# An encoder trunk on one core: the S5 scan in chunks of 16 tokens instead of 8, with values, gates and queries placed anew

## The chip, the cores and the metric

The kernel runs on one core of a Trainium2 chip. The metric is the device time of one execution in microseconds, the median of several runs. A core has a matrix engine (TensorE, PE in the profile, with PEld for its weight loads), three engines for elementwise work (VectorE, DVE; ScalarE, ACT; GpSimd, POOL) and SyncE (SP), which here only issues transfers. Transfers are issued from the queues of SP and POOL.

## The reference

One layer of a hybrid encoder runs over 2304 tokens: two sequences of 256 and 2048 tokens, each scanned on its own. All data is float32.

```
h = rmsnorm(x, norm1_g);  q, zf_f, zf_b, vi, g, u = split(h @ w_in)      # 1024 -> 3072
ya = hgrn2(q, zf_f, zf_b, vi, g)          # 4 heads of 128, gated linear recurrence, both directions
# S5: u in 32 groups of 16 channels, 64 complex states per group, both directions
bu = u @ Bbar;  x_t = Abar * x_{t-1} + bu_t;  y = Re(C x_fwd) + Re(C x_bwd) + d*u
z = gelu(y);  yb = norm(z * sigmoid(z @ glu_w + glu_b)) * merge_g
x = x + concat(ya, yb) @ w_out
x = rmsnorm(x + relu(rmsnorm(x) @ w_ff1)**2 @ w_ff2)
```

## The kernel before

Tokens go in six blocks of 384. A float32 product is made of three products of split operands (hi x hi, hi x lo, lo x hi; `mm3`, lines 174 to 179); the S5 and table products are plain float32 matmuls, which show as two passes each. The order of the instructions on each engine is set when the kernel is built: a planner simulates the engines and always takes the ready instruction that comes first in the program, so that later work can fill a hole of earlier work. `order` adds an edge that holds one instruction behind another; `hold[0]` does so for every `tt` on VectorE that is traced while it is set.

Stage 1 (lines 499 to 537) loads x, norms and transposes a block (`stage1_norm`), stores h split in two halves to DRAM, and projects u (`stage1_proj`, four output tiles of 128 channels per block, each 24 matmuls of 384 columns). `s5_tables` (277 to 497) works out on VectorE the powers of Abar and, in eight calls of `quad` for four groups each, three tables that go through DRAM: `win_d` (u to chunk-end state; transposed on TensorE), `wc_d` (state to output) and `k_d` (u to output inside a chunk, 15 lags; products of `bb` and `wc` on TensorE, line 486). A chunk is LC = 8 tokens, so that a matmul contracts 8 x 16 channels = 128 rows and its columns are the 288 chunks. `QD` says behind which block's norm which calls of `quad` stand. Of the values only block 5 is projected here (V1 = 5).

The entry of the scan (583, `s5_in`): for each of 32 groups two matmuls (real and imaginary), 128 rows, 288 columns, forward and backward states in two halves of the output partitions, copied by ACT (forward) and DVE (backward) into the state tiles `stt_`. The scan (589 to 595): in each round `s5_step` runs once for each direction, three VectorE operations a step: a product with `adec`, and two sums. For the first 30 rounds a step handles both sequences at once. Beside the scan run the values of blocks 0 to 4 (`stage2_v`, h loaded again by `load_h`), then gates and queries of blocks 0 to 3 (`stage2_gq`, eight units of 24 matmuls per block). The exit (638 to 658) makes, for each group, three matmuls of 288 columns into one bank: the table `tm` from `k_d` on u, and two of `wc` on the copied states `xg`; ACT evacuates, POOL stores.

Then the gate stage (716 to 763): gelu on ACT and DVE, a GLU product per block, with gates and queries of blocks 4 and 5 (`late`) placed between by `LN`. The gated recurrence, the output projection and the MLP follow and are the same in both kernels.

Of the kernel before, what the change touches and what calls it, by code (L numbers as in the profile page):

```python
# [9 lines left out]
F32 = mybir.dt.float32  # L10
# [24 lines left out]
JP = NPROMPT // LC  # L35
# [9 lines left out]
def hybrid_trunk_kernel(  # L45
# [80 lines left out]
    win_d = [dram.tile([P, 4, P], F32, name=f"win_d{i}") for i in range(G // 2)]  # L126
    wc_d = [dram.tile([P, 2, 4, LC * C16], F32, name=f"wc_d{o}") for o in range(8)]
    k_d = [dram.tile([4, C16, 15 * C16], F32, name=f"k_d{o}") for o in range(8)]
# [52 lines left out]
    def proj_fm(o, wu, hh, hl):  # L181
        for k in range(KD):
            mm3(o, wu[0][:, k], wu[1][:, k], hh[k // 4][:, k % 4], hl[k // 4][:, k % 4], k == 0, k == KD - 1)
# [74 lines left out]
    def stage1_proj(b):  # L258
        hh, hl = hx[b]
        for f in range(4):  # L260
            pu = ptile("mm", TB)
            proj_fm(pu, uw[f], hh, hl)
            ut = tmp.tile([P, LC, JB], F32, name="ut", tag="ut")
            act(ut, pu.rearrange("p (j i) -> p i j", i=LC), AF.Copy)
            GP.dma_start(out=u_d[f].rearrange("i f j -> f i j")[:, :, b * JB:(b + 1) * JB], in_=ut)

# [10 lines left out]
    def s5_tables():  # L277
        GQ = 4
# [78 lines left out]
        ap = par.tile([P, 2, 10, G], F32, name="apow")  # L357
# [21 lines left out]
        pw1 = par.tile([P, 4, G], F32, name="pw1")  # L379
        pw2 = par.tile([P, 4, G], F32, name="pw2")  # L380
# [7 lines left out]
        adec = []  # L388
        for d in range(2):
            ad = const.tile([P, 2, 2, G // 2], F32, name=f"adec{d}")  # L390
            for q in range(2):
                o, i = ad[q * 64:(q + 1) * 64], ap[d * 64:(d + 1) * 64, :, LC, q::2]
# [4 lines left out]
            adec.append(ad)  # L397
# [19 lines left out]
        pin = par.tile([P, 2, G, LC], F32, name="pin")  # L417
        for i in range(LC):
            V.tensor_copy(out=pin[:64, :, :, i], in_=ap[:64, :, LC - 1 - i, :])
            V.tensor_copy(out=pin[64:, :, :, i], in_=ap[64:, :, i, :])  # L420
        pout = par.tile([P, 2, G, 10], F32, name="pout")
        for e in range(10):
            V.tensor_copy(out=pout[:64, :, :, e], in_=ap[:64, :, 9 - e, :])
            V.tensor_copy(out=pout[64:, :, :, e], in_=ap[64:, :, e, :])

        dcol = par.tile([32, G // 2], F32, name="dcol")
        nc.sync.dma_start(out=dcol, in_=s5_d[0].rearrange("(a b) -> b a", b=32))
        idc = par.tile([32, C16], F32, name="idc")
        tt(idc, ident[:32, 0:16], ident[:32, 16:32], ALU.add)
# [5 lines left out]
        pb = [par.tile([P, GQ * 10 * C16], F32, name="s1", tag="s1", bufs=2)[:, :G * C16].rearrange("p (g c) -> p g c", g=G) for _ in range(2)]  # L435
        cmul(bb[:, 0], bb[:, 1], cb[0], cb[1], br[:, 0], br[:, 1], pb[0], pb[1])
        for ri in range(2):
            pr = ptile("tb", 512)
            for o in range(4):
                T.transpose(pr[:, o * P:(o + 1) * P], ldc[ri][:, o].rearrange("g d p -> g (d p)"), ident)  # L440
            act(cT[:, ri].rearrange("p g c -> p (g c)"), pr, AF.Copy)
        def quad(o):
            gs = slice(GQ * o, GQ * (o + 1))
            s1 = par.tile([P, GQ * 10 * C16], F32, name="s1", tag="s1", bufs=2)
# [7 lines left out]

            ws = par.tile([P, 2, GQ, LC, C16], F32, name="ws", tag="ws", bufs=2)
            sv = s1[:, :GQ * LC * C16].rearrange("p (g i c) -> p g i c", g=GQ, i=LC)
            cmul(ws[:, 0], ws[:, 1], b4(bb[:, 0], LC), b4(bb[:, 1], LC), p4(pin[:, 0], LC), p4(pin[:, 1], LC), sv, sv)
            for gp in range(GQ // 2):
                pw = ptile("tb", 512)
                for q in range(2):
                    for ri in range(2):
                        T.transpose(pw[:, (2 * q + ri) * P:(2 * q + ri + 1) * P], ws[:, ri, 2 * gp + q].rearrange("p i c -> p (i c)"), ident)  # L460
                wt = tmp.tile([P, 4, P], F32, name="wt", tag="wt")
                act(wt, pw.rearrange("p (a b) -> p a b", a=4), AF.Copy)
                GP.dma_start(out=win_d[GQ // 2 * o + gp], in_=wt)

            s2 = par.tile([P, GQ * 10 * C16], F32, name="s1", tag="s1", bufs=2)
            wc = par.tile([P, 2, GQ, 10, C16], F32, name="wc", tag="wc", bufs=2)
            sv = s2.rearrange("p (g i c) -> p g i c", g=GQ, i=10)
            cre, cim = b4(cT[:, 0], 10), b4(cT[:, 1], 10)
            pre, pim = p4(pout[:, 0], 10), p4(pout[:, 1], 10)
# [6 lines left out]
            GP.dma_start(out=wc_d[o], in_=wc[:, :, :, 1:9, :].rearrange("p r g i c -> p r g (i c)"))  # L476

            kt = par.tile([32, 2, 2, 15, C16], F32, name="kt", tag="kt", bufs=2)
            for gp in range(GQ // 2):
                g0 = GQ * o + 2 * gp  # L480
                pk = []
                for d in range(2):
                    pkd = ptile("tb", 256)
                    e0 = 2 if d == 0 else 0
                    for ri in range(2):
                        T.matmul(pkd[:32], bb[d * 64:(d + 1) * 64, ri, g0:g0 + 2].rearrange("p g c -> p (g c)"),
                                 wc[d * 64:(d + 1) * 64, ri, 2 * gp:2 * gp + 2, e0:e0 + 8, :].rearrange("p g i c -> p g (i c)"),
                                 start=ri == 0, stop=ri == 1)
                    pk.append(pkd[:32].rearrange("p (g i c) -> p g i c", g=2, i=8))
                act(kt[:, gp, :, 0:8], pk[0], AF.Copy)  # L490
                act(kt[:, gp, :, 8:15], pk[1][:, :, 1:8], AF.Copy)
                tt(kt[:, gp, :, 7], kt[:, gp, :, 7], pk[1][:, :, 0], ALU.add)
                stt(kt[:, gp, :, 7], idc.unsqueeze(1).to_broadcast([32, 2, C16]), dcol[:, g0 // 2:g0 // 2 + 1], kt[:, gp, :, 7], ALU.mult, ALU.add)
            for q in range(2):
                GP.dma_start(out=k_d[o].rearrange("(a q) c l -> q c a l", q=2)[q],
                             in_=kt[q * 16:(q + 1) * 16, :, q].rearrange("c a l e -> c a (l e)"))
# [3 lines left out]
    adec, quad = s5_tables()  # L500
    uw = [col_unit(w_in, 2560 + f * P) for f in range(4)]
    stage1_norm(1)
    onorm = col_load("onorm", hgrn_onorm_g[0], NH)
    glub = col_load("glub", s5_glu_b[0], 4)
    mergeg = col_load("mergeg", s5_merge_g[0], 4)
    stage1_proj(0)


    V1 = 5
    NE = 4  # L510
    NL = 2
    MK = 24

    def v_proj(b, hh, hl, out_tile, tag="fl"):
        for t in range(NCB):
            pv = ptile(tag, 512)
# [7 lines left out]
    QD = [[], [], [0, 1], [2, 3], [4, 5], [6, 7]]  # L524
    for b in range(1, NB):
# [6 lines left out]
        if b == max(V1 - 1, 1):  # L532
            wv = [row_unit(w_in, 256 * i, 1536, wx if i < 2 else None) for i in range(4)]
        stage1_proj(b)
        if b >= V1:
            v_proj(b, *hx[b], lambda: tmp.tile([P, D], F32, name="xt", tag="xt", bufs=6)[:, :512], "mm")
# [11 lines left out]
    stt_ = [sp.tile([P, NJ + 1, 2, GH], F32, name=f"st5_{d}") for d in range(2)]  # L548
    st2 = ExitStack()
    tmp2 = st2.enter_context(tc.tile_pool(name="tmp2", bufs=2, reuse_waits="tile"))  # L550
    wg = [col_unit(w_in, 2048 + h * P) for h in range(NH)]

    def s5_in(g):
        if g % 2 == 0:
            wt = tmp2.tile([P, 4, P], F32, name="wt", tag="wt")
            nc.sync.dma_start(out=wt, in_=win_d[g // 2])
            hx["wt"] = wt
        wt = hx["wt"]
        ug = tmp2.tile([P, NJ], F32, name="ug", tag="ug", bufs=4)
        nc.sync.dma_start(out=ug, in_=u_d[g // 8][:, (g % 8) * C16:(g % 8 + 1) * C16, :])  # L560
        for ri in range(2):
            pi = ptile("mm" if (2 * g + ri) % 5 < 3 else "sx", NJ)
            hx["mark", g] = T.matmul(pi, wt[:, 2 * (g % 2) + ri], ug, start=True, stop=True)
            qs = slice((g % 2) * 64, (g % 2 + 1) * 64)
# [3 lines left out]
    SL = 2 * GH  # L568

    def s5_step(d, src, dst, nq):  # L570

        gap = (JP if d == 0 else NJ - JP) * SL
        s0, d0 = (src * SL, dst * SL)
        prev = view(stt_[d], s0, [[gap, nq], [0, 2], [1, SL]])
        cur = view(stt_[d], d0, [[gap, nq], [1, SL]])
        swp = view(stt_[d], d0, [[gap, nq], [GH, 2], [1, GH]])
        pr = tmp2.tile([P, 2, 2, SL], F32, name="pr", tag=f"pr{d}")[:, :nq]
        ad = view(adec[d], 0, [[0, nq], [SL, 2], [1, SL]])
        tt(pr, prev, ad, ALU.mult)
        tt(cur, cur, pr[:, :, 0], ALU.add)  # L580
        tt(swp, swp, view(pr, SL + GH, [[2 * SL, nq], [-GH, 2], [1, GH]]), ALU.add)

    for g in range(G):
        s5_in(g)
    for j in (0, JP):
# [767 lines left out]
```

## Time and profile before

| | us |
|---|---|
| median of 3 runs (2757.64 to 2767.97) | 2758.93 |
| the profiled execution, its own time | 2759.81 |
| its span, first to last instruction | 2758.0 |
| PE busy in the span | 2623.8 (95%) |
| DVE busy | 1970.5 (71%) |
| ACT busy | 1432.8 (52%) |
| POOL busy | 411.6 (15%) |

The times of the rows below are from the profiled execution, counted from the start of its span. Matmul records overlap, since matmuls are pipelined: a busy PE is not yet a PE at its full rate. The rate is read from the distance of starts.

### The profile page before, as it was taken

How to read it: one execution, taken by the hardware profiler on the slowest of the kernel's cores; microseconds unless marked ns; L12 is line 12 of the kernel's file. 1: busy time of each engine (PE TensorE's matmuls, PEld its weight loads, DVE VectorE, ACT ScalarE, POOL GpSimd, SP SyncE). 2: the span in 40 equal slices, each digit the busy share in tenths (PEclk: the TensorE clock that was granted, in tenths of full speed). 3: DMA queues.
4: the chain of work that ended last, by engine and by line, in shares of the span. 5: the costliest groups of instructions: out<-in, count | busy, mean ns of one | idle time of the engine just before them, and what ended most of it. 6: DMA issues, size and time to landing. Idle time of an engine off the chain costs nothing.

```text
span 2758.0 us, 48707 instructions
## 1 busy us (share of the span) xinstructions
PE 2623.8 (95%) x17590; PEld 2355.9 (85%) x17590; DVE 1970.5 (71%) x5515; ACT 1432.8 (52%) x2632; POOL 411.6 (15%) x677
## 2 busy tenths in 40 slices
PE   6897999889999998999899999999999999999998
PEld 6774899679999887887899999999998888888887
DVE  6666879658799788565898787797765455555564
ACT  5535121477688676344676565676654334344342
POOL 1231223233111111222122011111110000000000
PEclk9998999999999999999999999999999999999999
DMA  9857654587646556799789798898787555775662
GB/s 264 253 189 225 206 202 141 175 245 210 216 148 215 179 184 217 248 342 334 285 310 326 253 330 302 303 344 320 293 319 272 176 174 169 245 238 191 196 218 81
DMA packets 352728, 657.58 MB, mean 238 GB/s; under 512 B 67656, under 2 KB 230856, under 8 KB 346344
## 3 DMA queue, kind: packets, MB, share of 16 engines
q1 hardware_dynamic: 280728, 353.72, 39.6%
q0 software_dynamic: 71760, 300.76, 30.1%
q8 instruction: 139, 2.28, 0.3%
q14 instruction: 101, 0.83, 0.1%
HBM read 434.97 MB, written 219.38 MB: 237 GB/s over the span
## 4 chain that ended last, share of the span: by engine, by line
PE 56%; issue 17%; DVE 11%; DMA 9%; POOL 4%; ACT 2%; SPq 1%; POOLq 0%; DVEq 0%; ACTq 0%
PE pm L175 7%; PE pm L178 7%; PE pm L179 7%; PE px_f L175 4%; PE px_f L178 4%; PE px_f L179 4%; DVE st L68 3%; PE px_g L179 3%; PE px_g L175 3%; PE px_g L178 3%; PE px_tr L178 2%; PE px_tr L179 2%; PE px_tr L175 2%; DMA w1r<-in_w_ff_dram 2%; DVE pr L68 2%
## 5 line engine op out<-in xcount | busy, mean ns | idle before, releaser
L68 DVE TENSOR_TENSOR sl<-gt,sh 128x1280 fp32r<-128x1280 f32 (+1 forms) x112 | 152.1, 1358 | 292.0 <-ACT sh L83 290.1
L83 ACT ACTIVATE sh<-gt 128x1280 fp32r<-128x1280 f32 (+1 forms) x112 | 130.8, 1168 | 394.0 <-PE pm L178 159.3
L175 PE MATMUL pm<-oh,w 128*128 128x384 f32 x672 | 227.5, 340 | 10.5 <-ACT oh L83 9.0
L179 PE MATMUL pm<-oh,w 128*128 128x384 f32 x672 | 227.8, 339 | 2.4 <-DVE w L68 2.4
L175 PE MATMUL px_f<-oh,w 128*128 128x384 f32 x672 | 227.0, 338 | 2.2 <-ACT oh L83 2.2
L178 PE MATMUL pm<-ol,w 128*128 128x384 f32 x672 | 227.8, 339 | 0.4 <-DVE ol L68 0.4
L179 PE MATMUL px_f<-oh,w 128*128 128x384 f32 x672 | 227.6, 339 | 0.0
L178 PE MATMUL px_f<-ol,w 128*128 128x384 f32 x672 | 227.3, 339 | 0.0
L175 PE MATMUL pm<-hh,whi 128*128 128x384 f32 x576 | 199.9, 350 | 8.1 <-ACT sg L83 3.8
L178 PE MATMUL pm<-hl,whi 128*128 128x384 f32 x576 | 200.9, 349 | 0.0
L179 PE MATMUL pm<-hh,wlo 128*128 128x384 f32 x576 | 197.7, 345 | 0.0
L83 ACT ACTIVATE sel<-KQ 128x384 f32<-128x384 f32 (+1 forms) x312 | 168.6, 559 | 50.5 <-DVE KQ L68 48.7
L68 DVE TENSOR_TENSOR KQ<-KQ,Fl 128x384 f32<-128x384 f32 x288 | 154.3, 552 | 10.8 <-ACT sel L83 8.8
L83 ACT ACTIVATE w<-w1t 128x512 fp32r<-128x512 f32 x192 | 120.2, 628 | 78.4 <-PE pm L179 43.0
L68 DVE TENSOR_TENSOR st<-st,pr 128x32 f32<-128x32 f32 (+1 forms) x1016 | 150.0, 202 | 0.0
L175 PE MATMUL pm<-th,sh 128*128 128x512 f32 x384 | 149.7, 391 | 0.0
L178 PE MATMUL pm<-tl,sh 128*128 128x512 f32 x384 | 149.4, 389 | 0.0
L179 PE MATMUL pm<-th,sl 128*128 128x512 f32 x384 | 149.4, 389 | 0.0
L83 ACT ACTIVATE c<-c 128x384 f32<-128x384 f32 x192 | 100.0, 523 | 86.5 <-DVE c L68 86.1
L68 DVE TENSOR_TENSOR w<-w1t,w 128x512 fp32r<-128x512 f32 x192 | 131.1, 684 | 17.3 <-ACT w L83 14.3
L175 PE MATMUL px_g<-th,sh 128*128 128x512 f32 x368 | 143.2, 389 | 0.0
L178 PE MATMUL px_g<-tl,sh 128*128 128x512 f32 x368 | 143.2, 389 | 0.0
(366 smaller groups left out, 7460.0 us busy)
## 6 DMA issues: line engine op xcount, KB each, us to landing
gt<-s_d SPq DMA_DIRECT2D x112, 384.0 KB
xg<-in_w_ff_dram SPq DMA_DIRECT2D x80, 512.0 KB
s_d<-his POOLq DMA_DIRECT2D x48, 768.0 KB, 7.7
hh<-h_hi POOLq DMA_DIRECT2D x46, 768.0 KB, 7.4
hl<-h_lo POOLq DMA_DIRECT2D x46, 768.0 KB, 6.7
w1t<-t_d SPq DMA_DIRECT2D x32, 1024.0 KB
xg<-t_d SPq DMA_DIRECT2D x64, 512.0 KB
s_d<-hid POOLq DMA_DIRECT2D x48, 576.0 KB, 4.7
```

Source lines behind the costliest of these rows:

```text
L68: ins = V.tensor_tensor(out=o, in0=a, in1=b, op=op)
L83: S.activation(out=o, in_=i, func=f, **kw)
L175: ins = T.matmul(o, ah, bh, start=first, stop=False)
L178: T.matmul(o, ah, bl, start=False, stop=False)
L179: return T.matmul(o, al, bh, start=False, stop=last)
```

## The change

- A chunk of the scan has SC = 16 tokens (144 chunks). u keeps its layout of 8 tokens; a matmul handles every second column of it, and two of them (SH = 2) make a chunk.
- Tables: `quad` is called 16 times, for two groups each, with 16 instead of 8 powers, 18 instead of 10, and 31 instead of 15 lags. `win_d` and `wc_d` double in total; the products for `k_d` go to four tiles of the array by `tile_position`. Eight of its 20 copies per table become one with four dimensions.
- Entry: the states lie in one tile, both directions. Per pair of groups 16 matmuls of 144 columns, on two column tiles of 64, fill one bank with both directions and groups; one copy of 128 partitions empties it (ACT for real, DVE for imaginary parts).
- Scan: where one sequence is left, one step of three operations handles both directions.
- Exit: per group seven matmuls: one of 288 columns, two of 144 (lags across the half chunks), four of 144 (states). Both copies of states are on DVE, all u loads on SP, more buffers, five banks instead of three.
- Stage 1 projects the values of all blocks, behind u of the same block; the tables' VectorE work is held behind the second block's norm, and their transposes behind u of block 0; `uw` and `wv` are loaded ahead of the tables' parameters.
- Gates and queries: block 0 is spread over the entry, blocks 1 to 3 stand beside the scan, block 4 is spread over the exit; only block 5 is left to the gate stage (NL = 1, `LN` smaller).

```diff
-        GQ = 4
+        GQ = 2
-        for base, n in ((1, 1), (2, 2), (4, 4), (8, 1)):
+        for base, n in ((1, 1), (2, 2), (4, 4), (8, 8), (16, 1)):
...
+            ws = par.tile([P, 2, GQ, SC, C16], F32, name="ws", tag="ws", bufs=2)
+            cmul(ws[:, 0], ws[:, 1], b4(bb[:, 0], SC), b4(bb[:, 1], SC), p4(pin[:, 0], SC), p4(pin[:, 1], SC), sv, sv)
+            for h in range(SH):
...
+                        T.transpose(pw[:, (2 * q + ri) * P:(2 * q + ri + 1) * P], ws[:, ri, q, h * LC:(h + 1) * LC].rearrange("p i c -> p (i c)"), ident)
+                GP.dma_start(out=win_d[o][:, h], in_=wt)
...
+            for ri in range(2):
+                for d in range(2):
+                    for r in range(2):
+                        T.matmul(pk[d][r * 32:(r + 1) * 32], bb[...], wc[...],
+                                 start=ri == 0, stop=ri == 1, tile_position=(d * 64, r * 32))
...
     stage1_norm(0)
-    adec, quad = s5_tables()
     uw = [col_unit(w_in, 2560 + f * P) for f in range(4)]
     stage1_norm(1)
+    wv = [row_unit(w_in, 256 * i, 1536, wx if i < 2 else None) for i in range(4)]
     stage1_proj(0)
-    V1 = 5
-    NL = 2
+    NL = 1
+    hold[0] = hx["lo", 1]
+    adec, quad = s5_tables()
+    for o in (0, 1):
+        quad(o)
+    hold[0] = None
+    stage1_v(0)
-    QD = [[], [], [0, 1], [2, 3], [4, 5], [6, 7]]
+    QD = [[], [2, 3, 4], [5, 6, 7, 8, 9], [10, 11, 12, 13, 14], [15], []]
...
         stage1_proj(b)
-        if b >= V1:
-            v_proj(...)
+        stage1_v(b)
...
         for ri in range(2):
-            pi = ptile("mm" if (2 * g + ri) % 5 < 3 else "sx", NJ)
-            hx["mark", g] = T.matmul(pi, wt[:, 2 * (g % 2) + ri], ug, start=True, stop=True)
-            act(stt_[0][qs, 1:NJ + 1, ri, g // 2], pi[:64], AF.Copy)
-            V.tensor_copy(out=stt_[1][qs, 0:NJ, ri, g // 2], in_=pi[64:])
+            for d in range(2):
+                for h in range(SH):
+                    for q in range(2):
+                        T.matmul(pi[q * 64:(q + 1) * 64, d], wt[:, h, 2 * q + ri, d * 64:(d + 1) * 64], ug[q][:, h::SH],
+                                 start=h == 0, stop=h == SH - 1, tile_position=(0, q * 64))
+            if ri:
+                V.tensor_copy(out=o, in_=pi)
+            else:
+                act(o, pi, AF.Copy)
...
+    gq = [stage2_gq(b, tmp2) for b in range(NB - NL)]
+    for g2 in range(GH):
+        s5_in(g2)
+        if g2 % 2:
+            next(gq[0], None)
...
+            f, b = JP + k, NS + NC2 - k
+            s5_step(f, f + 1, b - f, b - f - 2, view(adec, 0, [[2 * SL, 2], [SL, 2], [1, SL]]))
-    for b in range(V1):
-        stage2_v(b, hx["mark", MK] if b == 0 else None)
+    for g in gq[:-1]:
+        for _ in g:
+            pass
...
-        (nc.sync if g % 3 else GP).dma_start(out=ug, in_=u_d[o][:, q * C16:(q + 1) * C16, :])
+        nc.sync.dma_start(out=ug, in_=u_d[o][:, q * C16:(q + 1) * C16, :])
-        act(xg[:64], stt_[0][qs, 0:NJ, :, g // 2].rearrange("p j r -> p r j"), AF.Copy)
+        for d in range(2):
+            V.tensor_copy(out=xg[d * 64:(d + 1) * 64], in_=stt_[qs, d, d:NC2 + d, :, g // 2].rearrange("p j r -> p r j"))
+        T.matmul(py, tm[:, P:2 * P], uh, start=True, stop=False)
+        T.matmul(py[:, 1], tm[:, :P], uh[:, 0], start=False, stop=False)
+        T.matmul(py[:, 0], tm[:, 2 * P:], uh[:, 1], start=False, stop=False)
+        for h in range(SH):
+            for ri in range(2):
+                T.matmul(py[:, h], wc[:, ri, g % 2, (1 - h) * P:(2 - h) * P], xg[:, ri], start=False, stop=h == 1 and ri == 1)
+        if g % 4 == 0:
+            next(gq[-1], None)
...
-    for _ in range(9):
+    for _ in range(5):
         next(late, None)
-    LN = [2, 2, 2, 1, 1, 0]
+    LN = [1, 1, 1, 0, 0, 0]
```

## Rows read from the trace of the kernel before

**Rows 1.** The page, part 1: busy us (share of the span) x instructions of each engine.

```profile
PE 2623.8 (95%) x17590; PEld 2355.9 (85%) x17590; DVE 1970.5 (71%) x5515; ACT 1432.8 (52%) x2632; POOL 411.6 (15%) x677
```

**Rows 2.** Stretches: us, busy PE, PEld, DVE, ACT, POOL, PE clock, DMA share, GB/s.

```profile
0.00:100.00 100.00, 70.32 (x364) 63.19 (x364) 60.28 (x300) 57.64 (x92) 15.14 (x29) 0.93 0.86 253
100.00:221.00 121.00, 117.85 (x630) 91.28 (x631) 88.33 (x172) 51.71 (x101) 45.66 (x69) 0.97 0.68 216
221.00:287.00 66.00, 50.33 (x173) 34.08 (x173) 36.61 (x66) 36.67 (x63) 5.38 (x10) 0.90 0.69 218
287.00:511.00 224.00, 220.26 (x1154) 205.87 (x1153) 204.65 (x1482) 39.15 (x70) 62.77 (x99) 0.99 0.53 182
511.00:585.00 74.00, 54.34 (x197) 36.19 (x195) 27.75 (x84) 51.77 (x66) 26.10 (x41) 0.95 0.72 214
585.00:697.00 112.00, 110.31 (x636) 109.99 (x637) 83.82 (x142) 79.55 (x166) 37.60 (x52) 0.98 0.80 229
```

**Rows 3.** Timeline of PE, projections: start us, us, instruction; four and nine starts apart.

```profile
118.85 0.33 PE L175 MATMUL pm<-hh,whi 128*128 128x384 f32 x1
...
119.54 0.33 PE L178 MATMUL pm<-hl,whi 128*128 128x384 f32 x1
...
291.39 0.39 PE L175 MATMUL px_fl<-whi,hh 128*128 128x512 f32 x1
...
293.43 0.40 PE L175 MATMUL px_fl<-whi,hh 128*128 128x512 f32 x1
```

**Rows 4.** Timeline of PE in stage 1: table transposes and table products.

```profile
121.09 0.82 PE L460 MATMUL px_tb<-ident,ws 128*128 128x128 f32 x6
...
217.69 3.38 PE L486 MATMUL px_tb<-wc,bb 64*32 64x256 f32 x16
```

**Rows 5.** Timeline of PE in the scan's exit, three matmuls (six passes) apart.

```profile
546.02 0.65 PE L653 MATMUL pm<-ug,tm 128*128 128x288 f32 x2
...
547.48 0.65 PE L653 MATMUL pm<-ug,tm 128*128 128x288 f32 x2
```

**Rows 6.** Waits of PE from 508 to 700 us: total, times, longest.

```profile
PE pm L654 <- DMA wc<-wc_d: 8.7, 8, 2.6
PE pm L654 <- ACT xg L83: 6.9, 2, 6.0
```

**Rows 7.** Groups of PE from 585 to 690 us: count, busy us, mean ns, idle before.

```profile
L175 PE MATMUL px_fl<-hh,whi 128*128 128x384 f32 x104 | 35.7, 343 | 3.8 <-ACT gt L83 3.8
```

**Rows 8.** Timeline of DVE in the scan: two sequences, then one.

```profile
290.40 0.48 DVE L68 TENSOR_TENSOR pr<-st,adec 128x128 f32<-128x128 f32 x2
...
291.36 0.48 DVE L68 TENSOR_TENSOR pr<-st,adec 128x128 f32<-128x128 f32 x2
...
501.12 0.35 DVE L68 TENSOR_TENSOR pr<-st,adec 128x64 f32<-128x64 f32 x2
...
501.85 0.36 DVE L68 TENSOR_TENSOR pr<-st,adec 128x64 f32<-128x64 f32 x2
```

**Rows 9.** Groups of DVE by form from 285 to 515 us.

```profile
L68 DVE TENSOR_TENSOR st<-st,pr 128x64 f32<-128x64 f32 x120 | 18.4, 208 | 0.0
L68 DVE TENSOR_TENSOR pr<-st,adec 128x128 f32<-128x128 f32 x60 | 14.3, 274 | 0.0
```

**Rows 10.** Timeline of SP's queue: the first weight loads.

```profile
16.12 1.12 SPq L159 DMA_DIRECT2D st<-in_w_in_dram  x2
```

**Rows 11.** Groups of DVE in the first 221 us: two of the six for tables.

```profile
L68 DVE TENSOR_TENSOR s<-cT,pout 128x640 f32<-128x640 f32 x16 | 13.0, 813 | 0.0
...
L68 DVE TENSOR_TENSOR s<-bb,pin 128x512 f32<-128x512 f32 x16 | 10.9, 684 | 0.2
```

**Rows 12.** Timeline of PE in the recurrence: matmuls on 32 and 64 columns of the array.

```profile
726.49 0.57 PE L869 MATMUL px_at<-sel 128*64 128x64 f32 x12 [0.75 <-ACT sel L83]
726.98 0.45 PE L179 MATMUL pm<-hh,wlo 128*128 128x384 f32 x1
...
780.06 1.10 PE L862 MATMUL px_lv<-sel 128*32 128x32 f32 x88
```

More of the change, by code (lines that the diff above doesn't have):

```diff
@@ L34 @@
 JB = TB // LC
-JP = NPROMPT // LC
+SC = 16
+SH = SC // LC
+NC2 = NTOK // SC
+JP = NPROMPT // SC
+NE2 = SC + 2
+NLAG = 2 * SC - 1
 EPS = 1e-6
@@ L265, in stage1_proj @@
             GP.dma_start(out=u_d[f].rearrange("i f j -> f i j")[:, :, b * JB:(b + 1) * JB], in_=ut)
+        hx["u", b] = last
     def load_h(b, after=None):
@@ L475, in quad @@
             stt(wc[:, 1], wc[:, 1], -1.0, sv, ALU.mult, ALU.subtract)
[L476 to L481, printed above, removed]
+            GP.dma_start(out=wc_d[o], in_=wc[:, :, :, 1:SC + 1, :].rearrange("p r g i c -> p r g (i c)"))
+            kt = par.tile([64, NLAG, C16], F32, name="kt", tag="kt", bufs=2)
@@ L482, in quad @@
+            pk = [ptile("tb", SC * C16), ptile("tb", SC * C16)]
+            for ri in range(2):
                 for d in range(2):
-                    pkd = ptile("tb", 256)
                     e0 = 2 if d == 0 else 0
[L485 to L496, printed above, removed]
+                    for r in range(2):
+                        T.matmul(pk[d][r * 32:(r + 1) * 32], bb[d * 64:(d + 1) * 64, ri, GQ * o:GQ * o + 2].rearrange("p g c -> p (g c)"),
+                                 wc[d * 64:(d + 1) * 64, ri, r, e0:e0 + SC, :].rearrange("p i c -> p (i c)"),
+                                 start=ri == 0, stop=ri == 1, tile_position=(d * 64, r * 32))
@@ L579, in s5_step @@
+    def s5_step(src, dst, gap, gap2, ad):
+        prev = view(stt_, src * SL, [[gap * SL, 2], [0, 2], [1, SL]])
+        cur = view(stt_, dst * SL, [[gap2 * SL, 2], [1, SL]])
+        swp = view(stt_, dst * SL, [[gap2 * SL, 2], [GH, 2], [1, GH]])
+        pr = tmp2.tile([P, 2, 2, SL], F32, name="pr", tag="pr", bufs=4)
         tt(pr, prev, ad, ALU.mult)
         tt(cur, cur, pr[:, :, 0], ALU.add)
-        tt(swp, swp, view(pr, SL + GH, [[2 * SL, nq], [-GH, 2], [1, GH]]), ALU.add)
-    for g in range(G):
-        s5_in(g)
@@ L585, in hybrid_trunk_kernel @@
[L585 to L602 removed]
+        tt(swp, swp, view(pr, SL + GH, [[2 * SL, 2], [-GH, 2], [1, GH]]), ALU.add)
@@ L655, in hybrid_trunk_kernel @@
-        T.matmul(py, wc[:, 1, g % 2], xg[:, 1], start=False, stop=True)
+            wc = tmp3.tile([P, 2, 2, SC * C16], F32, name="wc3", tag="wc3", bufs=3)
+            nc.sync.dma_start(out=wc, in_=wc_d[g // 2])
+        tm = tmp3.tile([P, 3 * P], F32, name="tm", tag="tm", bufs=4)
+        kd = k_d[g // 2]
+        nc.sync.dma_start(out=tm, in_=bass.AP(tensor=kd.tensor, offset=kd.offset + g % 2 * 48 * NLAG * C16,
+                                              ap=[[C16, LC], [NLAG * C16, C16], [1, 3 * P]]))
@@ L658, in hybrid_trunk_kernel @@
         GP.dma_start(out=s5y_d[o][:, q * C16:(q + 1) * C16, :], in_=yg)
+        if g % 4 == 0:
+            next(gq[-1], None)
+        if g == G - 8:
+            hlate = {NB - NL: load_h(NB - NL)}
+    for _ in gq[-1]:
+        pass
     st3.close()
+    st2.close()
     s5s.close()
```

167 lines of the change are left out of this document (72 added, 95 removed).

## Prediction

> **What bounds the kernel now.** I read the busy table first. TensorE (PE) is busy 2623.8 us, 95% of the span of 2758.0 us [rows 1], so time can only come from the few places where PE has nothing to do, or from PE work itself. The profiled execution took 2759.81 us, 1.8 us outside its span and 0.9 us above the median of 2758.93 us; I sum against it and carry the result over as it is.
>
> The second view, the table by stretches [rows 2], says where those places are. Everything that the change touches lies before about 697 us. There PE stands idle 30 us of the first 100 (DMA share 0.86, 253 GB/s, granted clock 0.93), 16 of 66 in the scan's entry (221 to 287), 20 of 74 in its exit (511 to 585), and nearly nothing in the scan (287 to 511), where VectorE (DVE) is busy 205 of 224 us and PE 220.
>
> Busy time flatters PE, since the records overlap. So I priced PE by its pitch, from start to start. A pass of 384 columns takes (119.54 - 118.85)/4 = 0.1725 us, so one output tile of a projection (24 passes; a "unit" below) takes 4.14 us; a pass of 512 columns takes (293.43 - 291.39)/9 = 0.227 us, so values of one block (72 passes) take 16.3 us [rows 3]. A table transpose takes (0.82 - 0.28)/5 = 0.108 us, the 0.28 being the tail after the last start, and a table product (3.38 - 0.38)/15 = 0.200 us per pass [rows 4]. A full-size pass of the scan's matrices (288 columns, two passes per matmul) takes (547.48 - 546.02)/6 = 0.243 us, or 0.845 ns a column [rows 5]. Work against wall:
> - stage 1 (to 221): 24 units of u 99.4, one block of values 16.3, 216 transposes 23.3, 128 table passes 25.6 = 165; lost 56. The second stretch of it is almost full (117.9 of 121 [rows 2]), so most is lost in the first 100 us.
> - entry: 128 passes 31.1, 45 passes of values 10.2 = 41; lost 25.
> - scan: 315 passes of values 71.4, 35 units 145 = 216; lost 8 (3.5%).
> - exit: 192 passes 46.7; lost 27. Waits on wc loads (8.7 us) and on the states' copies (6.9 us, mostly the first group after the scan) lead there [rows 6].
>
> Of the scan's 35 units 32 belong to blocks 0 to 3 and 3 to the late gates and queries, of which 104/8 = 13 fall behind 585 us [rows 7].
>
> **The change, part by part.**
>
> **The scan's length** goes down and is worth nothing by itself. Before, a round of both directions takes 291.36 - 290.40 = 0.96 us with both sequences and (501.85 - 501.12) = 0.73 us with one [rows 8]. After, there are 14 rounds of the first kind and 112 merged steps of three operations that each need the one before. The upper price of a step is the sum of the durations, 0.274 + 2 x 0.208 = 0.69 us [rows 9]; the lower one, at the pitch of the interleaved operations, is 0.47. I take 0.69, since the chain is serial: 13 + 77 = 90 us instead of some 228. But PE was full under it. The cover after is 25 units, 104 us, and behind them block 4's 33 us; only from 1.1 us a step would the scan stick out.
>
> The page VectorE: DVE Perf Modes of the Trainium skill (section "The TRN2 errata") gives (N + 151)/0.96 ns for an fp32 tensor_tensor, 0.29 and 0.22 us here; the step would be 0.74 us and the scan 96 us, under the same cover. The rows' durations lie 5 to 7% lower, and decide.
>
> **Values in stage 1** move 5 x 16.3 = 82 us of PE work forward unchanged, and drop five reloads of h. What they fill is the point. Per block, stage 1 moves 1.5 MB of x, 3.0 of h and 0.75 of u; 5.25 MB at 253 GB/s [rows 2] are 20.8 us, against 16.6 us of u plus 2.6 of transposes on PE: transfers pace it. With values it is 35.5 us of PE against 6.0 MB, 23.7 us: PE paces. The tables' parameter loads, which hold the first weight load back to 16.1 us on SP's queue [rows 10], go behind uw, the second norm and wv. What stays lost: about 20 us until the first norm and weights are there, and some 10 for the slow clock and stray waits. 56 to 30 us, a gain of 26. The 15 added value stores and 24 added table stores wait on GpSimd's queue (POOL), which is busy 60.8 of 221 us; they also use x's ring of six tiles, which delays loads of x with a block in hand: nothing.
>
> **Tables** double. PE: 64 more transposes, 6.9 us; table passes go from 128 to 256, now on four tiles of the array. Serial that is +25.6 us, with two tiles at a time 0, with four -12.8. DVE: the row pairs stand for 48 operations of 512 elements (32.1 us) and 48 of 640 (38.5 us) [rows 11]; after, 96 of 512 and 96 of 576 elements (about 0.75 us, between the two), 138 us: +67. DVE's 148.6 of 221 us becomes 216 of some 283. I take no loss, because PE has values to run meanwhile; the other case is a rival.
>
> **Entry.** 256 matmuls of 144 columns on 64-column tiles: 512 x 144 x 0.845 ns = 62.3 us serial, 31.2 if both tiles always run together. The trace has such tiles: 12 passes of 64 columns at 128x64 have a pitch of (0.57 - 0.22)/11 = 0.032 us, and 0.041 with the change back to whole-array matmuls, against 0.054 serial; 88 passes at 128x32 take 0.0104 us against 0.027 [rows 12]. That is 1.3 to 1.7 times for two tiles and 2.6 for four. I take 40 us (+9; ends 0 and +31), and for the table products two at a time, 0. That u is now read with stride two has no row; I price it at nothing, its other end is a doubling of the strided passes, which I only keep in the range's upper end. Evacuation falls from 128 copies of 64 partitions to 32 of 128. Seven units (29 us) go between, and fill the waits: lost 25 to 8.
>
> Against this the Trainium skill has a rule: changing the tiling mode drains the engine (TensorEngine Tiling (Array Packing), section "Tiling Modes", "Key Properties"). Here the mode changes at every table and around every unit of the entry. The trace agrees in kind, with little weight: 0.041 against 0.032 us over 12 passes is 0.1 us a change; 100 changes would be 10 us, and the sum by the rule 2742.
>
> **Exit.** 1152 instead of 864 columns a group: 32 x 1152 x 2 x 0.845 ns = 62.3 us, +15.6. Block 4's gates and queries (8 units, 33 us) go between. Loads grow (tm threefold, wc twofold), about 27 MB in 103 us, just above the 253 GB/s of the start [rows 2], but partly fetched under the scan; all u loads are now on SP's queue, 11 off POOL's. Lost 27 to 8. All copies of states go to DVE, free by then.
>
> **The gate stage (585 to 697)** loses five units, 20.7 us. It can't shrink by all of it: DVE is busy 83.8 and ACT 79.6 of its 112 us [rows 2] in one chain per block, and PE's 91 would leave them no slack. I take 99 us (ends 92 and 107).
>
> **The sum.** Stage 1: 165 + 82 + 7 + 30 = 283 (rounded). Entry 40 + 29 + 8 = 77, to 360. Scan 104 + 3.5 = 107, to 467. Exit 62.3 + 33 + 8 = 103, to 570, where before stood at 585. Gate stage 99, to 669 against 697. The rest is untouched. So 28 us: 2760 - 28 = **2732 us**.
>
> **The rivals.**
> - *The tiles don't overlap (slower).* If 64-column tiles run one after the other, or drain at each change, the entry costs 62.3 and the tables 51.2 us: +22 and +26 over my terms, 2780 us. For it: the old table products alternate between two halves of the rows and show no overlap (0.200 us for 256 columns, where 0.216 is serial [rows 4, 5]). Against: [rows 12]. It decides from a joint price of 28 us, that is, below about 1.1 times.
> - *Tables on DVE pace stage 1.* They can't start before block 1's norm, about 45 us. From there DVE has some 200 us to do in order, and its waits on PE and ACT for tables repeat twice as often; the last norm would come near 265 and one block (33 us of PE) behind it: stage 1 ends at 299, 2748 us. For it: 76% mean load with norms queued among tables. Against: norms stand ahead of tables in the program.
> - *Holes vanish more fully.* Table products on four tiles (-13), gate stage at 92 (-7), entry at full overlap less a little: 2710 us.
> - *The shorter scan itself isn't the bound*, as argued; if the entry is paced by loads (13 MB and 3 of h), it is 90 us and 2745.
>
> **How the numbers follow.** The forecast with its own range of 2718 to 2746 gets 0.45, the fuller gain 0.20, tables on DVE or loads in the entry 0.20, tiles without overlap 0.15. The range goes to 2704 (fuller gain and cheap entry) and 2772 (half of the tile price and DVE together). About 0.5%, 13.8 us, is what a measurement here can tell from no change: below 2745 faster, above 2773 slower. That gives faster 0.41 + 0.19 + 0.03 = 0.63; same 0.22 from the upper part of the forecast, most of the DVE case and partial overlap; slower 0.15.
>
> **What would show it.** Right: the first value matmul soon after 40 us and PE nearly full from there; stage 1 over near 283 us; passes at 144 columns with a pitch near 0.08 us; a scan of about 90 us that ends before the units under it; the gate stage near 99 us with DVE busy 85% of it. Wrong: gaps of PE before transposes of x that end with DVE's tables; a pitch of 0.12 us in the entry; PE waiting for wt, wc or tm; a low granted clock in entry and exit; or a gate stage that keeps its 112 us.

## The result: slower by 1.0%, where 28 us were to be won

The changed kernel takes 2787.81 us (median; 2782.91 to 2792.71) against 2758.28 us of the kernel before beside it: a ratio of 1.0102, 95% interval 1.0068 to 1.0137. The forecast was 2732. The profiled execution took 2782.91 us; its span is 2781.1 us, against 2758.0 before, so the two profiles stand 23.1 us apart. PE is now busy 2648.9 us instead of 2623.8 [rows 1].

The table by stretches of the kernel after, with the columns of [rows 2], is cut at the ends of its stages: the start, the rest of stage 1 (to 297), the entry in two parts (to 400), the scan (to 531), the exit (to 612), the gate stage.

```profile
0.00:51.00 51.00, 28.35 (x144) 25.96 (x145) 23.63 (x74) 31.06 (x45) 6.14 (x16) 0.93 0.96 255
51.00:297.00 246.00, 244.49 (x1405) 197.65 (x1402) 190.20 (x474) 99.20 (x182) 79.01 (x125) 1.00 0.67 222
297.00:324.00 27.00, 20.80 (x98) 19.84 (x98) 2.53 (x4) 6.21 (x10) 4.93 (x8) 0.87 0.99 333
324.00:400.00 76.00, 73.22 (x719) 68.21 (x720) 10.80 (x16) 18.11 (x31) 13.89 (x20) 1.00 0.71 228
400.00:531.00 131.00, 131.00 (x757) 130.34 (x756) 108.22 (x429) 19.44 (x40) 36.77 (x56) 1.00 0.43 152
531.00:612.00 81.00, 64.24 (x422) 57.82 (x420) 23.59 (x58) 13.35 (x31) 18.93 (x31) 0.98 0.77 248
612.00:712.00 100.00, 91.50 (x505) 89.87 (x504) 84.33 (x148) 78.01 (x163) 26.87 (x39) 0.95 0.80 224
```

Set against the old table two things are to be seen. PE's holes are now gathered in three places: the first 51 us (PE busy for 28), the first 27 us of the entry (busy for 21) and the exit (busy for 64 of 81). And all of it ends late: the exit is over at 612 us, where before it was over at 585.

The first matmul of the recurrence's scores (px_lv) is the mark I go by from here. It comes at 722.5 us before and 726.9 after; the forecast puts it at 694.5. From there to the last px_lv it is 402.5 us before and 426 after, for the same instructions. So the result has two parts: 32 us of the forecast missing ahead of the mark, and 23 us lost in a stage that the change does not touch.

The second part shows in the waits of PE. The first block of lines is the kernel after, from 727 to 1152 us, the second the kernel before, from 722.5 to 1125 (what PE waited for, us in total, times, longest):

```profile
PE px_at L890 <- issue: 15.1, 7, 5.2
PE pm L184 <- issue: 4.5, 1, 4.5
PE pm L181 <- issue: 4.4, 1, 4.4
PE px_at L883 <- issue: 4.4, 3, 2.1
...
PE pm L185 <- issue: 1.7, 1, 1.7
```

```profile
PE px_at L869 <- issue: 5.8, 2, 4.2
PE px_at L862 <- issue: 4.0, 1, 4.0
PE px_at L869 <- ACT sel L83: 3.1, 5, 1.1
```

"Issue" means that no semaphore, engine or DMA in the profile explains the wait. It is 30.1 us in 13 stops after, 9.8 us in 3 before: 20 of the 23 us. The remaining 3 us may be the clock, which was granted at 0.97 there instead of 0.98, and lower right behind a stop (0.90 from 752.2 us on, in the stretches shown below); no run takes that apart.

The timeline of PE after, around the longest stop:

```profile
746.64 0.39 PE L890 MATMUL px_at<-sel 128*32 128x32 f32 x20
752.26 1.11 PE L890 MATMUL px_at<-sel 128*32 128x32 f32 x14 [5.24 <-issue]
```

The stop falls inside a run of equal matmuls, some 10 ns apart [rows 12]. I then counted PE's records from the start of the trace: weight loads, matmuls and PE's own semaphore instructions, 37,261 in all. The ten stops of more than 1 us come at records 9153, 9665, 10177, 10689, 11713, 12737, 13761, 15809, 18625 and 19649. Each of these numbers leaves 193 when divided by 256. The table by stretches, cut from one stop to the next in three places, shows it without counting by hand (the counts of PE and PEld are the first two in brackets):

```profile
752.20:767.62 15.42, 15.36 (x256) 14.67 (x255) 10.74 (x29) 11.56 (x25) 2.19 (x4) 0.90 0.35 123
784.30:798.30 14.00, 13.91 (x255) 13.29 (x256) 11.99 (x31) 11.16 (x26) 3.22 (x6) 1.00 0.69 243
802.60:832.20 29.60, 29.53 (x511) 28.53 (x510) 22.25 (x61) 21.35 (x48) 4.33 (x8) 0.94 0.34 120
```

The first two rows have 255 and 256 records, 511 in all, and with one semaphore instruction 512, twice 256; the third row has 1021, and with three of them 1024. The page's queue table names what comes in such blocks:

```profile
q8 instruction: 145, 2.38, 0.3%
```

That is 145 packets of 16,384 bytes, and 37,261 records are 145.6 times 256: PE's program comes in blocks of 256 instructions. In the stop at 747 to 752 us the packet starts at 749.83 and takes 0.96 us, and PE goes on 1.5 us after it. That holds for each of these stops in the six kernels of the table below, 56 in all: PE goes on 1.2 to 1.6 us after such a packet has ended. Not every wait for "issue" is of this kind: the two in the exit (2.0 us, shown further below) leave other numbers than 193 and follow no packet.

The Trainium skill (Runtime: NRT & Kernel Launch, section "Instruction fetch mechanics") says that instructions are refilled in blocks of 256. The packets agree. It adds that the fetch is hidden, since instructions are dispatched more slowly than they come in. The stops don't agree. One burst of the recurrence is 90 small matmuls of two passes with two instructions each, 360 instructions, and where nothing comes between them PE runs through it in 2 us (1.9 to 2.1 us in three of the bursts).

### The profile page after: what moved, and what is told of

Its sections match the earlier page's. It is cut to its first block, busy times and chain, and to the rows that moved or that the text cites. A ratio compares the mean times of both kernels' runs of the same rounds, so it can differ in the third digit from the quotient of the medians.

```text
span 2781.1 us, 49183 instructions
## 1 busy us (share of the span) xinstructions
PE 2648.9 (95%) x18422; PEld 2397.5 (86%) x18422; DVE 1911.9 (69%) x4467; ACT 1379.0 (50%) x2568; POOL 403.7 (15%) x670
## 4 chain that ended last, share of the span: by engine, by line
PE 80%; issue 7%; DMA 6%; DVE 2%; ACT 2%; POOL 1%; SPq 1%; POOLq 0%; DVEq 0%; ACTq 0%
PE pm L181 12%; PE pm L184 12%; PE pm L185 12%; PE px_f L184 4%; PE px_f L181 4%; PE px_f L185 4%; PE px_g L184 3%; PE px_g L185 3%; PE px_g L181 3%; PE px_tr L184 2%; PE px_tr L185 2%; PE px_fl L185 2%; PE px_fl L184 2%; PE px_fl L181 2%; PE px_tr L181 2%
## 5 line engine op out<-in xcount | busy, mean ns | idle before, releaser
L185 PE MATMUL px_g<-th,sl 128*128 128x512 f32 x368 | 143.2, 389 | 0.0
```

What stands on the lines that cost most here:

```text
L185: return T.matmul(o, al, bh, start=False, stop=last)
```

## Experiments on the recurrence: where the borders fall

Theory 1: the 23 us are such fetches, and what counts is where the borders of the blocks fall in the bursts, that is, how many instructions stand ahead of them. Theory 2: the planner placed the instructions of the recurrence in another order, which costs the time by its waits. Four kernels shift the program on PE at its very start, where PE waits for x, and leave the order of every other instruction on every engine as it was. An extra product is four records, two passes with a weight load each. The edit in the kernel after (32 of them, then 64) and, in the same place, in the kernel before (24, then 54):

```diff
         for k in range(KD):
             pt = ptile("tr", TB)
+            if b + k == 0:
+                for _ in range(32):
+                    T.matmul(pt[:32, :32], ident[:, :32], ident[:, :32], start=True, stop=True)
             for t in range(NCB):
```

> The kernel after, with 32 extra 32x32 products ahead of its first transpose, where PE waits for x anyway; every other instruction stands in the same order on every engine. They shift the program on PE by 128 records, half a block of 256. Theory 1 (instruction blocks: in the trace of after each of the ten long stops in the recurrence comes at a PE record whose number is 193 modulo 256, right behind a 16,384-byte packet of kind instruction, when a burst of 32-column matmuls has run through a whole block): the burst is now cut by the block's border, the stops of the recurrence fall from about 28 us to about 8, and the time from 2788 to 2766 (2760 to 2774). Theory 2 (the order of the recurrence, its waits for other engines): nothing changes, 2788 and the ten stops stay. The stretch before 727 us is the same by both.

> The kernel after with 64 extra products in the same place, which is a shift by 256 records, a whole block. Theory 1: the borders fall on the same instructions as in after, so the stops stay and the time is 2788 (2781 to 2795). Theory 2: 2788 too. If any small shift of the program or of its start moves the stops, both fall: then this one differs from after by 10 us or more.

> The kernel before, with 24 extra products at its start, a shift by 96 records; order otherwise the same. Before has three stops of this kind in the recurrence (10 us). Counting through its trace how fast PE gets through each block, theory 1 expects the borders to fall as badly as they can: some 20 places, 25 to 40 us more, so 2784 to 2799 (2787 as the point). Theory 2: 2758, no change.

> The kernel before with 54 extra products, a shift by 216 records, which by the same count is the best place: one short stop left instead of three. Theory 1: 2751 (2747 to 2755), 7 us under before. Theory 2: 2758.

Measured, with the waits for "issue" between the first and the last px_lv summed up from each kernel's own rows:

| kernel | shift in records | "issue": us, stops | first to last px_lv, us | time, us | ratio to before |
|---|---|---|---|---|---|
| after | 0 | 30.1, 13 | 426 | 2787.81 | 1.0102 [1.0068, 1.0137] |
| after_p32 | 128 | 7.8, 4 | 400.6 | 2778.53 | 1.0057 [1.0038, 1.0076] |
| after_p64 | 256 | 29.5, 14 | 426.2 | 2793.65 | 1.0110 [1.0091, 1.0129] |
| before | 0 | 9.8, 3 | 402.5 | 2762.73 | 1 |
| before_p24 | 96 | 30.6, 19 | 430.7 | 2785.12 | 1.0080 [1.0065, 1.0096] |
| before_p54 | 216 | 5.5, 3 | 395.2 | 2756.57 | 0.9983 [0.9970, 0.9996] |

(The kernel before stands with its median of the runs beside the four; beside after it was 2758.28.)

```profile
PE px_at L872 <- issue: 28.4, 18, 3.5
```

This is the longest of the rows of before_p24: the old kernel, with its order untouched, has caught the same loss, at 18 places that all leave 193 again. Half a block takes 25 us out of the recurrence of the kernel after; a whole block changes nothing; 96 records cost the kernel before 28 us there and 22 in all. Theory 1 is shown, and theory 2 falls for the 23 us: 400.6 us with the new order is no longer than 402.5 with the old one.

Two times missed their ranges. before_p54 came 6 us below the kernel before where 7 were expected, but at 2756.57 instead of 2747 to 2755, since the kernel before itself stood 4 us higher beside it. after_p32 was expected at 2766 (at most 2774) and came to 2778.53. Its first 400.6 us of the recurrence were as expected, but from the last px_lv to the last backward product it took 89 us against 80 in after, with one more border stop, of 4.7 us, and a wait for DVE of 3.5 us there. Behind that the rest of the kernel took 1563 us in its profile and 1549 in that of after, for the same instructions. This rest takes 1549 to 1568 us in the 14 profiles of this document, and why was not followed up; so the experiments below are better read at the mark than by their times.

From the first px_lv to the last backward product it is 478.6 us before, 505.3 after, 489 in after_p32, and 478 to 488 in the six later kernels with a good shift and all of the work. So up to 10 us of the recurrence may still hang on its order; that was not taken apart.

What is left with good borders on both sides is +0.6% (after_p32) against -0.2% (before_p54). Of the 28 us between these two profiles only 4 lie ahead of the mark, in what the change touches; 13 lie from there to the last backward product and 11 behind it, and no run shows what all of these are. So with the borders set aside the change is still no gain, and how much of a loss it is stays open. The 28 us that were forecast are missing ahead of the mark.

## Experiments ahead of the recurrence

All kernels from here on but one (values_alone) carry 34 to 36 extra products, a shift of 136 to 144 records, and are read at the mark, to be compared with 726.8 us of after_p32.

**Loads.** The entry's first wt was issued at 317 us, behind loads for the exit.

```diff
-            nc.sync.dma_start(out=wc, in_=wc_d[g // 2])
+            order(nc.sync.dma_start(out=wc, in_=wc_d[g // 2]), hx["in"])
```
Here hx["in"] is the entry's last load of u; tm, ug3 and the weights loaded from there on are ordered in the same way.

> The kernel after, with every load for the exit and the gate stage ordered behind the entry's last load on SP's queue, and 35 extra products at the start (140 records), so that the instruction borders fall well. In after the first wt was issued at 317 us, behind 3.5 MB of exit loads, and stage 1 ended at 297. Theory A (the entry lost its 17.6 us to these loads): first wt near 297 or before, the entry over near 390 instead of 399, and the first matmul of the recurrence at 719 instead of 726.8, as the units that the entry doesn't use lie under the exit. Rival (loads limited by their sum, the order doesn't matter): 727, unchanged. Time by theory A 2770, by the rival 2778, the time of the padded kernel after_p32.

The wt was issued at 297.4 us, as ordered, and nothing was won: the mark came at 737.7 us, 11 us later; 2773.49 us (1.0042 [1.0020, 1.0065]). PE then waited for that very load:

```profile
PE pm L581 <- DMA wt<-win_d: 8.5, 1, 8.5
```

From 297 to 306 us the queue of the h loads (POOL's, software_dynamic) moved 3.2 MB, and SP's (hardware_dynamic) 0.3 MB. The queue table from 303 to 308 us (packets, MB, share of the DMA engines) shows how:

```profile
q0 software_dynamic: 334, 1.77, 91.1%
q1 hardware_dynamic: 332, 0.17, 16.3%
```

The two queues took turns packet by packet, but nearly all packets of POOL's queue have 6,144 bytes there, and those of SP's 512. It was the same in after (474 packets each from 301 to 308 us). So the order on SP was not the cause; theory A falls.

**Cover.** Cover is PE work that can run beside a stretch in which another engine or the loads set the pace; here it is the units. Two kernels ask what the scan's length is worth.

```diff
         if g % 4 == 0:
+            behind[0] = end
             next(gq[-1], None)
+            behind[0] = None
```

Here `end` is the last product of the exit's group, and a unit's first matmul goes behind it, the units left over included.

> The kernel after with the gate and query units of block 4 held back until their group of the exit is done, and 35 extra products at the start. By the program order the scan now has 19.5 units (81 us) over it instead of 30.5, the exit 7 instead of 0, the gate stage 9 instead of 5. Theory B (the scan of 119 us, 0.845 us a step, used up the cover; PE work is only moved about): PE idles some 35 us at the end of the scan, the exit loses 8 instead of 23, the gate stage 1 instead of 9; first matmul of the recurrence near 740 (735 to 745), time 2791. Rival (the exit was bare only because of the order of issue): the exit's gain of 15 us shows in full, 712, and 2763.

The other one leaves out the second half of the scan:

```diff
-    for k in range(1, NC2 - JP - 1):
+    for k in range(1, (NC2 - JP - 1) // 2):
```

> The kernel after with the second half of the scan's steps left out, so its states and its output are not the reference's; 35 extra products at the start. The scan takes some 60 us instead of 119, and 19.5 units stand between entry and exit, 7 in the exit, 9 in the gate stage. Theory B (the step of 0.845 us instead of 0.69 is what cost the exit its cover): the scan ends under its units, the exit loses 8 us instead of 23, first matmul of the recurrence near 705 (700 to 710). Rival, my forecast's sentence that the scan's length is worth nothing below 1.1 us a step: 727, unchanged.

hold_units reached the mark at 735.1 us (2776.32 us, 1.0059 [1.0040, 1.0077]), half_scan at 700.1 (2742.15 us, one run). First the scan of hold_units, then the scan and the exit of half_scan:

```profile
401.00:517.00 116.00, 86.84 (x505) 85.75 (x501) 103.76 (x425) 14.07 (x29) 25.86 (x40) 0.89 0.38 131
```

```profile
400.00:483.00 83.00, 83.00 (x479) 82.47 (x478) 53.83 (x231) 13.35 (x27) 24.24 (x37) 1.00 0.39 136
483.00:578.00 95.00, 91.01 (x598) 86.11 (x598) 24.00 (x58) 19.18 (x43) 29.30 (x45) 1.00 0.85 272
```

With the units kept for the exit PE idles 29 us under the scan. With half the scan PE is full under it, and the exit, which has seven units now, is full as well (91 of 95 us). Half of the scan is worth 26.7 us at the mark, where the forecast's sentence gave it nothing. Theory B holds in both at the mark; the time of hold_units, expected at 2791, was 15 us below that.

**Values alone.** The kernel before, with the projection of values moved to stage 1 and the old scan (one line, `V1 = 5` to `V1 = 1`; no extra products):

> The kernel before with one part of the change alone: values of blocks 1 to 4 projected in stage 1 too (block 0 stays under the entry). The scan keeps its 8-token chunks and its 228 us on VectorE, but 288 of the 360 passes of values that stood in entry and scan are gone from there: the scan has 25 passes and 35 units over it, 151 us. Theory: stage 1 gains 20 us by the fill (ends at 266 instead of 221 + 65), the scan stretch stays at 228 and PE idles 77 of them; first matmul of the recurrence near 772 instead of 722.5, time 2807 (2795 to 2830). Rival (the scan's length isn't a bound, PE work is): 2738.

The mark came at 750.4 us, 28 later than before; 2796.27 us, 1.0130 [1.0101, 1.0160]. The time holds 9 us more of the recurrence too (412 us, with 16 us of "issue" stops). The sign and the mechanism are as expected (PE is busy for 152 of the 210 us from 336 to 546, under a scan that has lost its cover), the size at the mark is little more than half of what I expected. So the earlier values need the shorter scan; that the shorter scan by itself brings no gain was not tested.

**The entry without units.** If the units around the entry took the exit's cover, they should stand behind it.

```diff
+    behind[0] = hx["in", GH - 1]
     for g in gq[:-1]:
         for _ in g:
             pass
+    behind[0] = None
```
Here hx["in", GH - 1] is the entry's last product. The h of the first units comes in behind the entry's eighth pair, their weights and the exit's loads behind the entry's (in entry_bare_wg the gates' weights ahead of them).

> The kernel after, with no gate or query unit before the entry's last product: the units of blocks 0 to 3 are ordered behind it, their h comes in after the entry's eighth pair, their weights and the exit's loads stand behind the entry's loads on SP's queue; 36 extra products at the start (144 records) for good instruction borders. Theory C (in after the 12.7 units that ran around the entry, and the 6 MB of h that came in with its first loads, cost the exit its cover and drew the entry out from 297 to 399): the entry is 13 MB of loads at some 330 GB/s, 40 us, over at 340; the scan of 119 us runs under 29 units, to 462; the exit keeps 6 units and loses about 8; first matmul of the recurrence near 702 (697 to 712), time 2737 to 2750. Rival (PE work and the loads' sum set the end wherever the units stand): 727 and 2760. Second rival (the entry without units shows all its waits for loads, 60 us of it as before the change): near 720.

> As entry_bare, but the gate's four weight loads stand ahead of the entry's loads on SP's queue instead of behind them. Theory C: 2 MB more ahead of the entry (6 us), none to wait for behind it (4 us); the same within 5 us at the first matmul of the recurrence.

732.6 and 733.6 us at the mark; 2783.54 us (1.0078 [1.0056, 1.0100]) and 2784.43 us (1.0074 [1.0055, 1.0094]). Theory C falls. In entry_bare the exit was full, as it said, but the entry didn't shrink to 40 us: it took 81 for 33 us of products. The scan behind it grew, too, to 133 us from its first step to its last instead of 116 (127 in entry_bare_wg), since DVE now had the gates' weights to split beside its first rounds; but PE had no hole under it. The waits of SP in the entry say why it is long:

```profile
SPq L575 <- PE pm L581: 33.1, 8, 10.3
SPq L575 <- PE px_sx L581: 16.3, 5, 10.3
```

SP stands 49 us waiting for a free ug tile, with the next wt behind it. That led to theory D: the ring, the few tiles that the loads fill in turn, sets the pace by its round trip.

```diff
-        wt = tmp2.tile([P, SH, 4, P], F32, name="wt", tag="wt")
+        wt = tmp2.tile([P, SH, 4, P], F32, name="wt", tag="wt", bufs=4)
```
(ug 8 instead of 6; the room comes from the exit: wc3 2, tm 3, ug3 4)

> entry_bare with deeper rings for the entry's loads: wt 4 tiles instead of 2, ug 8 instead of 6, paid for by the exit's (wc3 2 instead of 3, tm 3 instead of 4, ug3 4 instead of 6). In entry_bare the entry took 81 us without any unit, for 33 us of products, and SP stood 49 us of it waiting for PE to free a ug tile with the next wt behind it. Theory D (the ring's round trip sets the entry's pace, not the bytes): the entry falls from 81 to 50 us or less, the scan starts by 347, first matmul of the recurrence at 702 to 712 instead of 732.6, time 2750 to 2763. Rival (bytes: 13 MB beside 3 MB of h): the entry stays near 80 and the time at 2780. If the exit pays for its shallower rings, that shows as waits for wc and tm there.

> The same rings in the kernel after (units may stand around the entry, the exit's loads ordered behind the entry's), 34 extra products at the start. By the program's order 4 units stand before the entry, 2 in it, 31 between entry and exit, 2 in the exit, 9 in the gate stage. Theory D: from 297 the entry needs 33 us of products, 25 of units and some 10 lost, so it ends near 365 instead of 399; the first matmul of the recurrence near 712 instead of 726.8, time 2763. Rival: the entry ends near 399 and nothing is gained, 2773.

ring_bare: the entry fell from 81 to 61 us, the scan started at 361.6, the mark came at 724.0, 2773.47 us (1.0042 [1.0027, 1.0057]). The ring is part of the pace: two thirds of what theory D expected of the entry, and less than half of it at the mark. ring_spread: the entry ended at 381 instead of 399, and the mark came at 733.6, 2787.01 us (1.0090 [1.0067, 1.0112]). There the exit paid. The longest waits of PE from 520 to 620 us:

```profile
PE pm L673 <- DMA wc<-wc_d: 5.3, 5, 1.4
PE px_sx L668 <- DMA tm<-k_d: 5.1, 6, 1.1
PE px_sx L673 <- DMA wc<-wc_d: 4.3, 3, 2.2
```

Of all versions with the change and the whole scan, none puts the mark earlier than 724 us. What one stretch gains, the next gives back: by the waits shown, entry and exit both run at the pace of their loads, and the units suffice for one of them beside the scan. Of the kernels with all of the work only before_p54, the old kernel with 54 idle products, was faster than before, by 0.2%.

## Why the prediction was wrong, step by step

**"The rest is untouched" is the step that decided the sign.** The instructions of the recurrence are untouched, their place in the program is not: 1,610 more PE records ahead of the first px_lv, six blocks and 74 records, moved every border in it. It cost 23 us between the first and the last px_lv. The rivals hold nothing of the kind. The trace of before had the clue, three "issue" waits of 9.8 us in bursts of small matmuls, two of them 4 us long, in a stretch that I had read only for its pitches [rows 12].

**The scan's step was taken 18% too short, and its cover was not free.** I took 0.69 us and called it the upper price. The timeline of DVE after, one step from start to start:

```profile
440.40 0.29 DVE L74 TENSOR_TENSOR pr<-st,adec 128x128 f32<-128x128 f32 x1
440.73 0.49 DVE L74 TENSOR_TENSOR st<-st,pr 128x64 f32<-128x64 f32 x2
441.25 0.29 DVE L74 TENSOR_TENSOR pr<-st,adec 128x128 f32<-128x128 f32 x1
```

The step is 0.846 us in the median. The durations that I used, 0.274 and 0.208 [rows 9], came from operations of two sequences in turn [rows 8]; in a chain the same forms take 0.29 and 0.225, and some 0.034 us lie between any two of them (the 0.49 above is two sums with such a gap). The Trainium skill's formula, which I cited and set aside (VectorE: DVE Perf Modes, section "The TRN2 errata"), gave 0.74: in the chain the trace agrees with it for both forms, and the three gaps, 0.10 us, are what it lacks.

That makes 108 us for the scan with its first 14 rounds. It took 117 instead of the forecast's 90, and the other 9 us are 12 steps of 1.5 to 1.7 us, in each of which one operation lasted 0.9 to 1.15 us. DVE and POOL at one of them:

```profile
459.83 1.15 DVE L74 TENSOR_TENSOR pr<-st,adec 128x128 f32<-128x128 f32 x1
```

```profile
459.82 1.02 POOL L604 TENSOR_TENSOR gt<-gt,sg 128x384 f32<-128x384 f32 x1 [8.92 <-ACT gt L89]
```

POOL multiplies the gates there, once for each gate unit. In after and in all nine kernels made from it each such product beside the scan meets one long operation of the scan, and no operation is that long without one. hold_units has 8 of them beside the merged steps, half_scan 4, and so 6.0 and 3.1 us instead of 9.0. The forecast has no term for it.

I wrote that the scan sticks out only from 1.1 us a step. That compared it with the units under it alone, and not with what those units were to cover next; half_scan prices half of the scan at 26.7 us.

**Entry.** The products cost less than I took. The timeline of PE after shows two runs of passes of 144 columns on two tiles:

```profile
344.77 2.27 PE L576 MATMUL px_sx<-ug,wt 128*64 128x144 f32 x32
346.86 2.27 PE L576 MATMUL pm<-ug,wt 128*64 128x144 f32 x32
```

It is 2.09 us from start to start, 0.065 us a pass against 0.122 serial and 0.08 in the forecast; the rival without overlap is dead. Nor does the stride of two, which I priced at nothing, show a cost here: 0.061 would be full overlap. The loss was mis-sized: some 16 us instead of 8 (102 us less 33 of products and 53 of units). 12.7 units ran there instead of 7, since the loads came late, and these units are the exit's missing cover. The load-paced entry was my fourth rival, at 90 us and 2745; it took 102.

**Exit.** The products are as forecast (58 us, and 5 more under the scan; I had 62.3), but 23 us are lost instead of 8. No unit was left for it. Waits of PE from 531 to 612 us:

```profile
PE pm L664 <- DMA tm<-k_d: 8.5, 5, 2.5
PE px_sx L664 <- ACT yg L89: 2.8, 2, 1.4
PE pm L664 <- issue: 2.0, 2, 1.8
PE px_sx L664 <- DMA tm<-k_d: 1.7, 2, 1.4
```

I had counted these loads "partly fetched under the scan"; rings of three wc and four tm tiles hold no more than the first groups' loads.

**Stage 1** ended at 297, not 283. It did what I argued: PE is full from 51 us on (244.5 of 246), so values pay for the transfers, and tables on DVE pace nothing. Waits of PE to 297 us:

```profile
PE px_tr L256 <- ACT xt L89: 18.0, 3, 17.2
PE px_tr L256 <- DVE lbt L74: 4.6, 1, 4.6
```

The first row is mostly the wait for the first block's norm, the second no table either: lbt is a small parameter of the recurrence, for whose load DVE stands 5.1 us, with the halves of h queued behind it. Of the 44 us lost instead of 30 some 23 lie in the first 51, where I had put about 20. The other 21, where I had put 10, lie where the records leave no gap, so passes ran slower than my pitch: counted over the whole stretch, those of 512 columns stand 0.249 us apart instead of 0.227 and those of 384 columns 0.183 instead of 0.1725, which is 14 us. What slows them I didn't test.

**Right were** the tables' products (8 passes in 1.05 us, twice overlapped, as I took).

**The gate stage** looks right by luck. I had 99 us and its stretch took 100, but it held five units instead of eight, since three more had been done by then, and its stretch is cut nearer to the mark (15 us ahead of it, 25.5 before). From the end of the exit to the mark it is 115 us, where the forecast implies 124.5.

The sum ahead of the mark: stage 1 +14, entry to exit 315 us instead of 287, +28, and -10 behind it: 32 us. With 23 in the recurrence, 3 from there to the last backward product and 8 less in the rest, that is the 51 us between 2732 and the profiled 2782.9, up to rounding. The 8 us are within what the rest differs from profile to profile.

**What stays open:** what slows stage 1's full stretch, how much of the entry's 61 us with deeper rings is bytes, and why the rest behind the recurrence differs by up to 19 us from profile to profile.

## What to carry over

An edit that adds or removes instructions on an engine moves the borders of its instruction blocks in all that follows; where bursts of short instructions run through a block faster than the next one comes, compare two kernels at several shifts before you credit or blame the edit. Cover is one account for neighbouring stages: price a serial stretch by what its cover would otherwise have covered. The cost of a dependent step is its pitch in a chain, not the sum of durations from interleaved chains; and look at what the other engines run beside it.

## What was not expected of the hardware

PE stopped for up to 5.2 us at the border of a block of 256 instructions (record 193 modulo 256, in the bursts of all the kernels of the table above). In bursts the packets of two blocks follow each other by 3.3 us at the least (729.54 and 732.86 us in after), against 1.3 us in which PE can run 256 instructions at 10 ns a pass. A shift of 96 records changed the old kernel by +0.8%, one of 216 by -0.2%.

Loads issued by POOL took nearly all that the DMA engines moved for 9 us (3.2 of 3.5 MB in loads_first), since the queues took turns by packets of 6,144 and of 512 bytes. And each product of two tiles on POOL, 1.0 us long, that ran beside the scan met a DVE operation that was 0.7 to 0.9 us longer than its like.
